# Moving weight splits, a residual and a few row splits to other places in a two-block fp32r kernel's issue order

## The chip, the cores and the metric

One core of a Trainium2 chip runs the whole program. The metric is the device time of one execution in microseconds (us); lower is better. Three runs of the kernel before took 2922.98, 2934.39 and 2939.07 us, so the time before is the median, 2934.39 us.

## What is computed

256 tokens of width 1024 go through two transformer blocks in float32. Block one has, in each of two layers, a SwiGLU feed-forward (`x = x + 0.5 * gate * swiglu(h)`, inner width 2816), a mixer (differential attention, then a gated recurrence) and a second feed-forward. Each normed input is scaled and shifted by columns that come from a conditioning vector:

```python
h = rms_norm(x, norm_g[layer, 0]) * (1.0 + scale[:, :, 0]) + shift[:, :, 0]
x = x + 0.5 * gate[:, :, 0] * swiglu(h, ffn_w_in[layer, 0], ffn_w_down[layer, 0])
```

Block two has a sliding-window attention, an expert layer over 16384 experts (each expert is a row of `u` and a row of `v`), a gated short convolution and a second expert layer. The ten stages are called ffn00, attn1, ffn01, ffn10, hgrn, ffn11, attn2, peer0, conv, peer1.

## The kernel before, in words

**Products.** x lies transposed, features on the partitions, in eight slices `xt[:, k]` of 128 features by 256 tokens. Each weight matrix comes in pieces of 128x1024 elements (512 KB). A piece is loaded by a DMA of SyncE's queue into a `raw` buffer and split into two fp32r halves: `whi`, a copy on ScalarE (ACT), and `wlo = raw - whi` on VectorE (DVE). The input is split in the same way into `xh` and `xl`. A product of one 128x128 block is three matmuls into one PSUM bank: whi by xh, whi by xl, wlo by xh (`mm3`, lines 652 to 657). `features` (898 to 911) multiplies one piece with all eight slices (24 matmuls) and gives one bank; `group` (802 to 812) does that for several pieces at once, slice by slice.

**When a piece is split.** Program order is fixed as the Python runs, and each engine works its instructions off in that order. `take(name, i)` (595 to 606) hands out the next piece. Before, it calls `proc_next` for as long as the pieces split are at most `self.ahead` past the one taken and there is a free pair of buffers. A feed-forward stage has six of those pairs, so with `ahead = 100` the pieces up to number c + 5 are split at the taking of piece c. Pieces are counted from 0 in each stage. `proc_next` (570 to 593) also works off what the plan puts between the pieces: the columns of the conditioning (the `ada_scr` operation on DVE, one per column of 128 values). In ffn00, ffn01 and ffn10 the plan has two of these to three pieces from piece 8 on, in ffn01 and ffn10 in the order 8, ada, 9, ada, 10, 11, ada, 12, ada, 13; ffn11 has none.

**Entering a stage of block one.** `enter` (864 to 884) computes the first six pieces while the norm is still being worked out. Pieces 0 to 3 are multiplied with the unnormed input (258 columns, two of them for the shift); meanwhile the sum of squares, the reciprocal root and its row `rs` are made, and with piece 3 the normed input is written slice by slice over the unnormed one (`norming`, 837 to 862). Pieces 4 and 5 use the normed input. `ahead` takes the four values of `AHEAD` in turn. With `AHEAD[3] = 1` the pieces 0 to 6 are split by the time that `group` has taken 4 and 5. After it `complete` (827 to 835) finishes the four unnormed products (`un`: a multiply and a copy on DVE, an add on ACT).

**The feed-forward.** `ffn` (968 to 1003) then makes the gated products of f = 0, 1, 2 (`glu`: silu on ACT into `sa`, the product `t` on DVE, its split `gh` on ACT and `gl` on DVE), and goes on with pieces 6 and 7 for f = 3 and so on. The banks go round: four for `features`, so piece n may start when the product of piece n - 4 has been read, and pieces 6 to 9 when the `un` of pieces 0 to 3 have been made.

**The residual behind a mixer.** `out_proj` (913 to 949) takes the last two pieces together and ends in `resids` (791 to 800), which for each of eight slices adds to `xt` (DVE), makes the unnormed `xh` (ACT) and `xl` (DVE), squares on ACT and adds the squares on DVE (`ss`). `rstd` (814 to 819) then has four short matmul records sum `ss` over the partitions. At the start of the program `squares_pe` (764 to 773) does it in another way: each squared slice goes to the PE by itself.

**The expert layer.** `peer` multiplies all 128 pieces of `u`, then takes the activations in `slots`, split by `halves` (663) into the eight buffers of `xh` and `xl`, as the input of the 128 pieces of `v`. The first four of these splits (`make(4)`, `make` at 1875) stand behind the last piece of `u`.

Of the kernel before, what the change touches and what calls it, by code (L numbers as in the profile page):

```python
# [19 lines left out]
T = 256  # L20
D = 1024
KD = D // P
# [61 lines left out]
LAST = 2  # L84
PEER_LAST = 3

AHEAD = (2, 3, 3, 1)

STAT = 4

# [248 lines left out]
def moving(pool, n, name):  # L339

    t = pool.tile([P, MOVE + n * T], F32R, name=name)
    return t[:, MOVE:].rearrange("p (a b) -> p a b", b=T)


class Kernel:
# [445 lines left out]
    def resids(self, acc, gate):  # L791

        y = lambda n: acc[n // 2][:, (n % 2) * T:(n % 2 + 1) * T]
        self.add(0, y(0), gate)
        for n in range(KD):
            if n < KD - 1:
                self.add(n + 1, y(n + 1), gate)
            if self.next is not None:
                self.unnormed(n)
                self.squares(n)  # L800

    def group(self, names, cols, role, each=None):

        w = [self.take(*x, n) for n, x in enumerate(names)]
        ps = [self.bank(role) for _ in names]
        for k in range(KD):
            if each is not None:
                each(k)
            for (h, l), p in zip(w, ps):
                self.mm3(p[:, :cols], h[:, k], l[:, k], self.xh[:, k, :cols], self.xl[:, k, :cols],  # L810
                         k == 0, k == KD - 1)
        return ps

    def rstd(self):
# [49 lines left out]
    def enter(self, names, dest):  # L864


        found = []

        def statistics(k):
            if k == STAT:  # L870
                found.append(self.rstd())
            elif k == KD - 1:
                self.rstd_rows(found[0])

        self.ahead = AHEAD[0]
        ps = self.group(names[:2], self.cols, "e", statistics)
        self.ahead = AHEAD[1]
        ps.append(self.features(*names[2], self.cols, "e"))
        self.ahead = AHEAD[2]
        normed = self.norming()  # L880
        ps.append(self.features(*names[3], self.cols, "e", each=normed))
        self.ahead = AHEAD[3]
        two = self.group(names[4:6], T, "n")
        self.ahead = 100
        return [self.complete(p, d) for p, d in zip(ps, dest)] + two
# [82 lines left out]
    def ffn(self, s):  # L968
        nc, wk = self.nc, self.wk
        layer, sub = SUB[s]  # L970
        self.banks(p=range(4), x=range(4, 8), e=range(4), n=[4, 5], ms=[6, 7])
        with self.tc.tile_pool(name=s, bufs=1) as pool:
            gh = moving(pool, KF, "gh")
            gl = moving(pool, KF, "gl")

            def glu(f, pa, pb):
                sa = pool.tile([P, T], F32, name="sa", bufs=2)
                nc.scalar.activation(sa, pa[:, :T], AF.Silu)
                g = wk.tile([P, T], F32, name="t", bufs=3)
                nc.vector.tensor_mul(g, sa, pb[:, :T])  # L980
                self.halves(gh[:, f], gl[:, f], g)

            un = [pool.tile([P, T], F32, name="un", bufs=4) for _ in range(4)]
            first = self.enter([(s + "_in", i) for i in range(6)], un)
            for f in range(3):
                glu(f, first[2 * f], first[2 * f + 1])
            for f in range(3, KF):
                pa = self.features(s + "_in", 2 * f)
                pb = self.features(s + "_in", 2 * f + 1)
                glu(f, pa, pb)  # L990
            nc.scalar.preload_act_table_set(LN_EXP)
            gt = self.gate(layer, sub, 0.5)
            if self.next is not None:
                self.lead(self.next)
            py = {}
            for i, (j, k) in enumerate(DOWN):
                if i % 8 == 0:
                    h, l = self.take(s + "_dn", i // 8)
                if k == 0:
                    py[j] = self.bank("x")  # L1000
                self.mm3(py[j][:, :T], h[:, i % 8], l[:, i % 8], gh[:, k], gl[:, k], k == 0, k == KF - 1)
                if k == KF - 1:
                    self.resid(j, py[j][:, :T], gt)
# [577 lines left out]
    def peer(self, s):  # L1581
# [3 lines left out]
        NJ, WAIT = 128, 1000.0  # L1585
        self.banks(p=range(4), x=range(4, 8), acc=range(4, 8), e=[4, 5, 6] if i == 0 else [1, 2, 3], ms=[7])
        with tc.tile_pool(name=s, bufs=1) as pool, tc.tile_pool(name=s + "g", bufs=2) as self.gp:
# [26 lines left out]
            nh, nl = (moving(spent, KD, n) for n in ("nh", "nl"))  # L1614
# [13 lines left out]
            first = self.group([(s + "_q", hp) for hp in range(3)], T, "e")  # L1628
# [157 lines left out]
            state = dict(j=0, t=0)  # L1786
# [16 lines left out]
            def steps():  # L1803
                yield from choose()
                state["chosen"] = True
                yield from build()
# [4 lines left out]
            def work(us):  # L1811
                credit[0] += us
                while credit[0] > 0.0:
                    c = next(gen, None)
                    if c is None:
                        return
                    if c == WAIT:
                        credit[0] = 0.0
                        return
                    credit[0] -= c  # L1820
# [15 lines left out]
            def slot(j):  # L1836
                j = ORDER[j]
                return slots[:, j] if j < P - N_SHARED else state["shared"][:, j - (P - N_SHARED)]

            def activate(j, ps):  # L1840
                t, x = state["t"], slot(j)
                if t < T:
                    nc.scalar.activation(x[:, t:], ps[:, t:T], AF.Gelu)
                if t:
                    e = wk.tile([P, T], F32, name="t", bufs=3)
                    nc.scalar.activation(e[:, :t], ps[:, :t], AF.Gelu)
                    v.tensor_mul(x[:, :t], x[:, :t], e[:, :t])
                state["j"] = j + 1

            for j in range(NJ):  # L1850
                work(BUDGET)
                while j >= J_FREE and "chosen" not in state:
                    work(1.0)
                if j == N_FREE - 3:
                    self.more = {}
                if j == N_FREE + 1:
                    assert max(max(self.parts[k, True]) for k in ("whi", "wlo")) < self.n_live
                    stack.close()
                    shared = stack.enter_context(tc.tile_pool(name=s + "s", bufs=1))
                    state["shared"] = shared.tile([P, N_SHARED, T], F32, name="shared")  # L1860
                    self.ahead = 100
                if 0 < j < 5:
                    for k in (2 * j - 2, 2 * j - 1):
                        nc.scalar.activation(self.xh[:, k, :T], nh[:, k].bitcast(F32), AF.Copy)
                        v.tensor_copy(self.xl[:, k, :T], nl[:, k].bitcast(F32))
                ps = self.features(s + "_u", j, x=(nh, nl) if j < 5 else None)
                self.after(2, lambda j=j, ps=ps: activate(j, ps))
                self.tick()
            while state["t"] < T:
                work(1.0)  # L1870
                self.tick()
            acc = [self.bank("acc") for _ in range(4)]
            made = [0]

            def make(upto):
                while made[0] < min(upto, NJ):
                    j = made[0]
                    self.halves(self.xh[:, j % 8, :T], self.xl[:, j % 8, :T], slot(j))
                    made[0] += 1

            def part(n, j, w):
                self.mm3(acc[n // 2][:, (n % 2) * T:(n % 2 + 1) * T], w[0][:, n], w[1][:, n],
                         self.xh[:, j % 8, :T], self.xl[:, j % 8, :T], j == 0 and n % 2 == 0, j == NJ - 1, skip=True)

            make(4)
            for j in range(NJ - PEER_LAST):
                self.tick()
                if j == 4:
                    self.drain()
                    nc.scalar.preload_act_table_set(LN_EXP)  # L1890
                if j == NJ // 2:
                    stack.close()
                    parts(PEER_LAST)
                make(j + 4)
                w = self.take(s + "_v", j)
                for n in range(KD):
                    part(n, j, w)
            if self.next is not None:
                self.lead(self.next)
            make(NJ)  # L1900
            w = [self.take(s + "_v", NJ - PEER_LAST + i, i) for i in range(PEER_LAST)]
            for n in range(KD):
# [9 lines left out]
    def build(self):  # L1912
# [5 lines left out]
        self.psum = pool("psum", 1, space=bass.MemoryType.PSUM)  # L1918
        self.banks(x=[4, 5, 6, 3], ms=[7])
        ctx.enter_context(tc.manual_schedule())  # L1920
        self.make_plan()
        self.ada_done = set()

# [35 lines left out]
        s = self.stages[0]  # L1959
# [114 lines left out]
```

## Time and profile before

| | us |
|---|---|
| median of three runs | 2934.39 |
| lowest, highest run | 2922.98, 2939.07 |
| the profiled execution, its own time | 2930.7 |
| its span, first to last instruction | 2928.9 |
| PE busy in the span | 2853.0 (97%) |
| DVE busy | 2177.9 (74%) |
| ACT busy | 1670.7 (57%) |

The profiled execution took 1.8 us more than its span, and 3.7 us less than the median. A matmul's record lasts about 0.28 us, but in a stream they start every 0.11 to 0.12 us, so a busy PE is an upper bound; how far apart they start tells more. In the timelines a row has the start, the duration, the engine, the operation, what is written and read, how many instructions are merged, and in brackets the idle time of the engine before it and what ended it.

### The profile page before, as it was taken

To read this page: it belongs to the slowest core of one execution; us is meant where nothing else is said; L and a number is where in the kernel's file an instruction comes from. 1 tells how busy PE (TensorE), PEld (TensorE's weight loads), DVE (VectorE), ACT (ScalarE), POOL (GpSimd) and SP (SyncE) were. 2 spreads that over 40 slices of the span, in tenths; PEclk is the share of its full clock that TensorE was granted. 3 is DMA by queue.
4 is the path that set the end of the run, shared out by engine and by line. 5 is a ranking of instruction groups with operands and counts; after the bars stand their busy time and mean duration, and the time that the engine had idled before them with its cause. 6 is when DMAs were issued, how large, how long until landed. Compare 5 with 4: busy or idle time off the path is not lost.

```text
span 2928.9 us, 61184 instructions
## 1 busy us (share of the span) xinstructions
PE 2853.0 (97%) x24416; PEld 2806.1 (96%) x24416; DVE 2177.9 (74%) x4491; ACT 1670.7 (57%) x3234; POOL 12.2 (0%) x20
## 2 busy tenths in 40 slices
PE   4999989999999999999999999999999999999999
PEld 4998889999999999799999999999999999999999
DVE  6876778878797655779889755656779889755554
ACT  4455654455465544664688655555464688654543
POOL 0000000000000000000000000000000000000000
PEclk9999999999999999999999999999999999999999
DMA  6984459879643554155544555656445544555654
GB/s 253 341 320 173 152 188 331 278 259 326 231 149 127 188 187 157 54 171 194 184 163 161 173 193 194 216 195 212 163 166 187 188 161 165 173 187 186 207 187 142
DMA packets 158990, 577.17 MB, mean 197 GB/s; under 512 B 17648, under 2 KB 19824, under 8 KB 158320
## 3 DMA queue, kind: packets, MB, share of 16 engines
q1 hardware_dynamic: 156096, 565.25, 56.4%
q0 software_dynamic: 1280, 6.30, 0.6%
q8 instruction: 191, 3.13, 0.4%
q10 hardware_dynamic: 1328, 1.71, 0.2%
q14 instruction: 95, 0.78, 0.1%
HBM read 570.57 MB, written 2.62 MB: 196 GB/s over the span
## 4 chain that ended last, share of the span: by engine, by line
PE 92%; DVE 4%; ACT 2%; issue 1%; DMA 1%; ACTq 0%; DVEq 0%
PE bank L249 92%; DVE wlo L249 1%; DVE xl L249 1%; ACT whi L249 1%; DVE t L249 1%; DMA params<-par 1%; ACT L249 0%; ACT un L249 0%; DVE ada_scr L249 0%; DVE ss L249 0%; DMA raw<-ffn_in 0%; DMA raw<-attn_qk 0%; ACT xh L249 0%; ACT gh L249 0%; ACT pk L249 0%
## 5 line engine op out<-in xcount | busy, mean ns | idle before, releaser
L249 PE MATMUL bank<-xh,whi 128*128 128x256 f32 (+1 forms) x6272 | 1775.9, 283 | 26.1 <-ACT whi L249 17.3
L249 PE MATMUL bank<-xh,wlo 128*128 128x256 f32 (+1 forms) x6272 | 1752.9, 279 | 4.0 <-DVE wlo L249 4.0
L249 PE MATMUL bank<-xl,whi 128*128 128x256 f32 (+1 forms) x6272 | 1755.8, 280 | 0.5
L249 DVE TENSOR_TENSOR wlo<-raw,whi 128x1024 fp32r<-128x1024 f32 x932 | 1134.3, 1224 | 540.5 <-ACT whi L249 532.7
L249 ACT ACTIVATE whi<-raw 128x1024 fp32r<-128x1024 f32 x932 | 973.3, 1057 | 704.0 <-PE bank L249 610.9
L249 PEld LDWEIGHTS bank<-xh,whi 128*128 128x128 f32 x6272 | 1187.9, 189 | 32.3 <-ACT whi L249 18.5
L249 PEld LDWEIGHTS bank<-xl,whi 128*128 128x128 f32 x6272 | 1194.4, 190 | 6.5 <-DVE xl L249 2.1
L249 PEld LDWEIGHTS bank<-xh,wlo 128*128 128x128 f32 x6272 | 1188.0, 189 | 5.4 <-DVE wlo L249 5.4
L249 PE MATMUL bank<-gh,whi 128*128 128x256 f32 x704 | 196.1, 278 | 0.0
L249 PE MATMUL bank<-gl,whi 128*128 128x256 f32 x704 | 196.1, 278 | 0.0
L249 PE MATMUL bank<-gh,wlo 128*128 128x256 f32 x704 | 196.1, 278 | 0.0
L249 DVE SCALAR_TENSOR_TENSOR ada_scr<-raw,cact 128x1024 f32<-128x1024 f32 x144 | 175.5, 1219 | 8.4 <-ACT cact L249 6.2
L249 ACT ACTIVATE ql<-q,gl 128x128 f16<-128x128 f16 x512 | 162.5, 396 | 0.0
L249 ACT ACTIVATE gh<-t 128x256 fp32r<-128x256 f32 x88 | 36.8, 418 | 190.7 <-DVE t L249 190.7
L249 PEld LDWEIGHTS bank<-gh,wlo 128*128 128x128 f32 x704 | 132.9, 189 | 0.0
L249 PEld LDWEIGHTS bank<-gl,whi 128*128 128x128 f32 x704 | 132.9, 189 | 0.0
L249 PEld LDWEIGHTS bank<-gh,whi 128*128 128x128 f32 x704 | 132.2, 188 | 0.0
L249 ACT ACTIVATE slots<-bank 128x256 f32<-128x256 f32 (+38 forms) x296 | 86.8, 296 | 16.7 <-PE bank L249 16.3
L249 PE MATMUL bank<-oh,whi 128*128 128x256 f32 x256 | 73.8, 288 | 0.2 <-ACT hx L249 0.2
L249 PE MATMUL bank<-qh,pm 128*128 128x128 f16 x512 | 73.0, 222 | 0.3
L249 PE MATMUL bank<-ql,pm 128*128 128x128 f16 x512 | 71.5, 219 | 0.1
L249 PE MATMUL bank<-ol,whi 128*128 128x256 f32 x256 | 71.6, 280 | 0.0
(235 smaller groups left out, 2551.4 us busy)
## 6 DMA issues: line engine op xcount, KB each, us to landing
raw<-peer_u SPq DMA_DIRECT2D x256, 512.0 KB, 3.3
raw<-peer_v SPq DMA_DIRECT2D x256, 512.0 KB, 3.4
raw<-ffn_in SPq DMA_DIRECT2D x176, 512.0 KB, 5.1
raw<-ada SPq DMA_DIRECT2D x144, 512.0 KB, 5.3
raw<-ffn_dn SPq DMA_DIRECT2D x88, 512.0 KB, 5.0
raw<-peer_q SPq DMA_DIRECT2D x32, 512.0 KB, 3.3
raw<-conv_in SPq DMA_DIRECT2D x24, 512.0 KB, 4.3
raw<-attn_qk SPq DMA_DIRECT2D x16, 512.0 KB, 4.7
```

The source lines that it names most:

```text
L249: result = real(*args, **kw)
```

## The change

It sets `AHEAD[3]` to 2. It gives the banks of a feed-forward stage in another order. It issues `glu(1)` and `glu(2)` behind the first piece of f = 3 and f = 4. Where a feed-forward follows a mixer, `resids` only adds slice 0 and leaves a function `feed`; `group` calls it in front of each slice of the stage's first two pieces, and the squares go to the PE slice by slice; the row `rs` is then made within piece 2. In the expert layer the first four rows of `v` are split within the last piece of `u`.

```diff
-AHEAD = (2, 3, 3, 1)
+AHEAD = (2, 3, 3, 2)
...
         self.add(0, y(0), gate)
+        if self.next is not None and self.next[0] == "f":
+            def feed(n):
+                if n < KD - 1:
+                    self.add(n + 1, y(n + 1), gate)
+                self.unnormed(n)
+                if n:
+                    self.squares_pe(n - 1)
+
+            self.feed, self.ss = feed, None
+            return
         for n in range(KD):
...
         w = [self.take(*x, n) for n, x in enumerate(names)]
         ps = [self.bank(role) for _ in names]
+        feed, self.feed = self.feed, None
         for k in range(KD):
+            if feed is not None:
+                feed(k)
             if each is not None:
                 each(k)
...
+        if feed is not None:
+            self.squares_pe(KD - 1)
         return ps
...
+        def rows(k):
+            if k == STAT:
+                self.rstd_rows(found[0])
+
         self.ahead = AHEAD[0]
-        ps = self.group(names[:2], self.cols, "e", statistics)
+        ps = self.group(names[:2], self.cols, "e", None if fed else statistics)
+        if fed:
+            found.append(self.rstd())
         self.ahead = AHEAD[1]
-        ps.append(self.features(*names[2], self.cols, "e"))
+        ps.append(self.features(*names[2], self.cols, "e", each=rows if fed else None))
...
-        self.banks(p=range(4), x=range(4, 8), e=range(4), n=[4, 5], ms=[6, 7])
+        self.banks(p=[2, 3, 0, 1], x=range(4, 8), e=[2, 3, 0, 1], n=[5, 7], ms=[4, 6])
...
-            for f in range(3):
-                glu(f, first[2 * f], first[2 * f + 1])
+            glu(0, *first[0:2])
             for f in range(3, KF):
                 pa = self.features(s + "_in", 2 * f)
+                if f < 5:
+                    glu(f - 2, *first[2 * f - 4:2 * f - 2])
                 pb = self.features(s + "_in", 2 * f + 1)
                 glu(f, pa, pb)
...
+            def early(k):
+
+                if state["t"] == T and k < 4:
+                    make(k + 1)
+
...
-                ps = self.features(s + "_u", j, x=(nh, nl) if j < 5 else None)
+                ps = self.features(s + "_u", j, x=(nh, nl) if j < 5 else None, each=early if j == NJ - 1 else None)
```

## Rows read from the trace of the kernel before

**Rows 1.** The page: the chain that ended last, by engine.
```profile
PE 92%; DVE 4%; ACT 2%; issue 1%; DMA 1%; ACTq 0%; DVEq 0%
```

**Rows 2.** The chain in order of time (start, us, what) behind five stage entries.
```profile
72.23 174.30 PE bank L249 x1480
...
423.65 174.88 PE bank L249 x1464
...
619.90 171.68 PE bank L249 x1493
...
806.46 113.92 PE bank L249 x868
...
974.73 186.73 PE bank L249 x1574
```

**Rows 3.** Timeline of PE in ffn10: piece 7 starts, then piece 12.
```profile
618.64 0.38 PE L249 MATMUL bank<-xh,whi 128*128 128x256 f32 x1 [4.06 <-ACT whi L249]
...
634.78 0.28 PE L249 MATMUL bank<-xh,whi 128*128 128x256 f32 x1
```

**Rows 4.** Timeline of ACT in ffn10.
```profile
609.28 0.51 ACT L249 ACTIVATE xh<-t,shift 128x256 fp32r<-128x256 f32 x1 [0.41 <-DVE t L249]
...
617.54 1.99 ACT L249 ACTIVATE whi<-raw 128x1024 fp32r<-128x1024 f32 x2
```

**Rows 5.** Timeline of DVE in ffn10.
```profile
610.29 0.42 DVE L249 TENSOR_TENSOR un<-bank,ss 128x256 f32<-128x256 f32 x1
...
618.62 2.36 DVE L249 TENSOR_TENSOR wlo<-raw,whi 128x1024 fp32r<-128x1024 f32 x2 [0.52 <-ACT whi L249]
620.89 1.22 DVE L249 SCALAR_TENSOR_TENSOR ada_scr<-raw,cact 128x1024 f32<-128x1024 f32 x1
```

**Rows 6.** Timeline of PE: piece 12 starts in ffn00, ffn01, ffn11.
```profile
87.83 0.28 PE L249 MATMUL bank<-xh,whi 128*128 128x256 f32 x1
...
439.75 0.28 PE L249 MATMUL bank<-xh,whi 128*128 128x256 f32 x1
...
990.13 0.28 PE L249 MATMUL bank<-xh,whi 128*128 128x256 f32 x1
```

**Rows 7.** Stretches: us, busy (x count) of PE, PEld, DVE, ACT, POOL; PEclk, DMA, GB/s.
```profile
619.50:622.90 3.40, 3.00 (x14) 3.00 (x15) 3.40 (x5) 2.87 (x4) 0.00 (x0) 0.50 0.51 188
...
807.20:810.60 3.40, 3.40 (x18) 3.40 (x18) 1.80 (x3) 2.95 (x5) 0.00 (x0) 0.50 0.85 275
```

**Rows 8.** Timelines between hgrn and ffn11: DVE, ACT, SP, PE.
```profile
939.74 0.87 DVE L249 SCALAR_TENSOR_TENSOR xt<-bank,gate,xt 128x256 f32<-128x256 f32 x2
...
957.03 0.87 DVE L249 SCALAR_TENSOR_TENSOR t<-xt,gain,ss 128x256 f32<-128x256 f32 x2
...
948.05 1.99 ACT L249 ACTIVATE whi<-raw 128x1024 fp32r<-128x1024 f32 x2
...
950.22 0.20 ACT L249 ACTIVATE rsq<-rsq 128x2 f32<-128x2 f32 x1
...
939.85 0.33 SPq L249 DMA_DIRECT2D raw<-ffn_in  x1
...
948.81 0.61 PE L249 MATMUL bank<-ones_d,ss 128*128 128x1 f32 x4 [3.12 <-DVE ss L249]
949.28 0.36 PE L249 MATMUL bank<-xh,whi 128*128 128x258 f32 x1
```

**Rows 9.** DMA issues from 933 to 946 us: KB each, median us to landing.
```profile
raw<-ffn_in SPq DMA_DIRECT2D x8, 512.0 KB, 4.1
```

**Rows 10.** Timeline of PE in hgrn (piece 7) and attn1 (piece 8).
```profile
805.20 0.39 PE L249 MATMUL bank<-xh,whi 128*128 128x256 f32 x1 [0.91 <-ACT whi L249]
...
273.21 0.58 PE L249 MATMUL bank<-xh,whi 128*128 128x256 f32 x1 [4.89 <-ACT hx L249]
```

**Rows 11.** Timeline of PE where peer0 goes from u to v.
```profile
1685.75 0.28 PE L249 MATMUL bank<-xh,whi 128*128 128x256 f32 x1
1686.16 0.38 PE L249 MATMUL bank<-xl,whi 128*128 128x256 f32 x1
```

More of the change, by code (lines that the diff above doesn't have):

```diff
@@ L864, in enter @@
     def enter(self, names, dest):
+        fed = self.feed is not None
         found = []
@@ L1848, in activate, with make @@
                 state["j"] = j + 1
+            made = [0]
+            def make(upto):
+                while made[0] < min(upto, NJ):
+                    j = made[0]
+                    self.halves(self.xh[:, j % 8, :T], self.xl[:, j % 8, :T], slot(j))
+                    made[0] += 1
+            def early(k):
+                if state["t"] == T and k < 4:
+                    make(k + 1)
             for j in range(NJ):
@@ L1872, in peer @@
             acc = [self.bank("acc") for _ in range(4)]
[L1873 to L1879, printed above, removed]
             def part(n, j, w):
@@ L1920, in build @@
         ctx.enter_context(tc.manual_schedule())
+        self.feed = None
         self.make_plan()
```

## The prediction, made before the change was run

> **What bounds the kernel now.** I began with the page's chain of waits, the work that ended last followed back: 92% of it is PE [rows 1]. In order of time it falls into long unbroken runs of matmuls: 1493 of them follow 619.90 in 171.68 us [rows 2], one each 0.115 us, so a piece of 24 takes about 2.75 us wherever PE is fed. What is to be won lies at the stage entries where a run breaks, and there I read the timelines engine by engine. In ffn10 piece 7 starts after an idle 4.06 us, released by its `whi` [rows 3], because ACT reaches that copy only at 617.54, behind the gated products, though the last normed slice was done at 609.79 [rows 4]; its `wlo` starts at 618.62 and ends about 1.2 us later [rows 5]. Behind the wait comes a second loss: for 3.4 us the granted clock is 0.50, which is 1.2 GHz, half of the upper level [rows 7]. Only 14 to 18 matmuls start there instead of some 29, about 1.7 us. Such an entry stands in ffn00, ffn01, ffn10 and ffn11, a smaller one (0.91 us, then 0.50 as well) in hgrn [rows 7, 10]. At the mixer's end PE waits 3.12 us for the last sum `ss` [rows 8].
>
> The sum below is on the profiled execution, 2930.7 us, 1.8 us over its span and 3.7 us under the median of the runs, 2934.39. I add the change to the median.
>
> **Part 1, piece 7 split early, products spread (four feed-forward entries).** I walk the two queues in ffn10. `whi` of piece 7 goes to 609.7-610.7 and `wlo` to 610.8-612.0. The first `un`, at 610.29 before [rows 5], thus moves by some 1.7 us, to 612.0, and piece 6, which needs its bank, waits under 1 us. Only `glu(0)` is left in front of piece 8: its `wlo` starts near 617.8 where before it was the second of the pair from 618.62, at 619.8 [rows 5], so the 4.06 us become about 0.9 at piece 8. So far this looks like nearly all won. But work is only moved on DVE, and DVE has six operations in its queue next: `wlo` of 8, a column of conditioning, 9, a column, 10, 11, each some 1.14 us apart (1.22 us long, overlapping) [rows 5]. The product `t` of `glu(1)`, which the change puts behind the first piece of f = 3, stands behind all six: 617.8 + 6.8 = 624.6. On ACT its `gh` waits for that `t`, and behind `gh` in ACT's order stand `whi` of 12 (1.0 us, half of [rows 4]) and the silu of f = 3, which frees the bank that piece 10 needs: 626.8. Piece 10 then waits about 2.5 us, and after two pieces more PE waits again, some 1.6 us, for the silu of f = 4. By this walk piece 12 starts at 633.95, against 634.78 before [rows 3]: a gain of 0.8 us only. DVE's backlog is late next, in place of ACT's `whi`.
>
> In the other entries I measure from the chain's break to piece 12: in ffn10 after the change 633.95 - 619.90 = 14.05 us. The two stages with the same two columns to three pieces get the same: ffn01 423.65 + 14.05 = 437.70 against 439.75, a gain of 2.05; ffn00 72.23 + 14.05 = 86.28 against 87.83, a gain of 1.55 [rows 2, 6]. ffn11 has no columns, so four of 1.22 us leave DVE's queue before piece 12 and the walk has it at 985.1 against 990.13 [rows 6]: 5.0. Together **-9.4 us**. The bounds: 0, if DVE's queue is longer than I count, and four times the stall and its slow clock, 4 x (4.06 + 1.7) = -23, if it never bites. I take the walk because each of its operations has a row.
>
> The new order of the banks costs nothing that I can find, as long as piece 6 follows the `un` of the bank it gets; the wait of under 1 us above is that.
>
> **Part 2, the residual in the first products (ffn01, ffn11).** Before, `resids` came whole, then the splits of pieces 2 and 3 (`whi` from 948.05) [rows 8]. Now `take` runs inside `group` right behind `add` of slice 0 and in front of all the rest. In ffn11 the raw of piece 3 was issued only at 939.85 and lands about 3.3 to 4.1 us later (the window's median is 4.1) [rows 8, 9], so `whi` runs 943.2-944.2, `wlo` to 945.4, and the second `add`, which stood at 940.2, waits behind it on DVE; on ACT `xh` of slice 0 waits behind `whi`. The first `xl` is ready at 946.3. From there the group is PE's own: 48 matmuls of 0.12 us and eight groups of sums, each of four short records. One such group took 0.47 us (948.81 to 949.28) [rows 8]. 48 x 0.12 + 8 x 0.47 = 9.6 us, ends 955.9. Behind it comes the root on ACT and DVE (before, 1.1 us from the sums' end at 949.28 to 950.42) [rows 8], the `whi` and two `wlo` of the next pieces (1.0 + 2.36 [rows 4, 5]) and then the first normed `t`: 960.3 against 957.03 before [rows 8], **+3.3**. The one wait of 3.12 us is gone, but another of about 3.7 us stands ahead of the group. After a wait of that size the clock fell to 0.50 elsewhere [rows 7], and here the slower stretch then lies under the longer group: +1.5 us. In sum +4.8 in each of the two stages, **+9.6**. ffn01 takes the same for lack of a nearer row; there only piece 3 is to be split. Bounds in each: -0.8 (below) and +5.6, with a landing of 4.1 instead of 3.3.
>
> The short records could be cheaper or dearer. The trace says 0.118 us each, as much as a matmul with 256 columns, and the sum uses that. The Trainium skill (TensorE: Matmul & The Clock Gate, Back-to-back issue gap) gives a moving side of 1 to 64 columns a floor of about 25 ns; by that a group would be an estimated 0.1 us and the two stages 5.9 us shorter.
>
> **Part 3, hgrn.** Piece 7 is split early there too, and no long DVE queue of conditioning lies behind it: 0.91 us of wait and 1.7 of slow clock go [rows 7, 10]: **-2.6** (bounds 0 and -2.6). **attn1**: PE waits 4.89 us for `hx` ahead of piece 8 [rows 10]; the extra early `wlo` (1.2 us) pushes it somewhat, bounds 0 and +1.2, I take a third, **+0.4**. attn2, conv and the query products keep their waits. **Part 4, v's first rows:** from u to v PE steps 0.41 us where it is usually 0.11 [rows 11]. Made within the last piece of u, ready on time, that is 0.3 to 0.4 in each expert layer: **-0.8** (bounds 0, -0.8).
>
> **Sum:** -9.4 + 9.6 - 2.6 + 0.4 - 0.8 = **-2.8 us**. So 2927.9 on the profiled scale, **2931.6** as a median. My own range for this case, by the bounds, is about 2919 to 2942. A measurement of this kernel can tell about 0.5% from no change, 14.7 us: faster is under 2919.7, slower over 2949.1.
>
> **Rivals.**
> (a) DVE's backlog does not bite, and the splits land ahead of the second `add`: all four stalls vanish with their slow clock, -23.2; hgrn -2.6, v -0.8; in each fed stage the 3.12 us wait and its 1.5 us go and 3.8 us of sums come, -0.8, two times -1.6. Sum -28.2, 2906.2. For: DVE is 74% busy overall. Against: six operations in a row at that place [rows 5]. Chance 0.15.
> (b) Only the residual goes well (raw of piece 3 already there): -9.4 - 1.6 - 2.6 + 0.4 - 0.8 = -14.0, 2920.4. For: the transfer may be issued earlier when buffers come free earlier. Chance 0.12.
> (c) Only the entries go well: -23.2 + 9.6 - 2.6 + 0.4 - 0.8 = -16.6, 2917.8. Chance 0.09.
> (d) Slower. In the fed stages the wait ahead of the group brings the clock down and PE, fed slice by slice, does not get it back through the two first pieces and piece 2. At 0.50 a matmul takes about 0.21 us (3.0 us busy for 14) [rows 7] instead of 0.12: 72 x 0.09 + 3.8 for the sums at half speed = 10.3, two times 20.6; 3.0 of it were in the forecast: -2.8 + 20.6 - 3.0 = +14.8, 2949.2. It decides if 0.50 lasts more than 10 us behind a wait. Against: the stretches that I see last 3.4. Chance 0.06.
> (e) A record with one moving column costs PE almost nothing, since it waits only for its issue: the 2 x 8 groups of 0.47 us [rows 8] drop out, 7.5 at most: -2.8 - 7.5 = -10.3, 2924.1. The row speaks against it. The Trainium skill's floor, named above, is this mechanism; the same page's section LDWEIGHTS (loading the stationary operand), where the price goes by the 128 columns loaded, an estimated 107 ns by its formula, agrees with the 118 ns of the row instead. Chance 0.03.
> That leaves 0.50 for the forecast and 0.05 for what I don't see.
>
> **Numbers.** Faster: (a) 0.15, half of (b) and (c), each near the bound, 0.11, and 0.04 of the rest: 0.30. Slower: half of (d) and some of the unseen, 0.05. Same 0.65. The range from 2906 to 2944 holds the forecast, (b), (c), (e) and half of (a).
>
> **What would show it.** Right: no wait on `whi` at piece 7; instead PE idle ahead of piece 10, released by ACT's silu, behind a `gh` that waits for a `t` of DVE. `wlo` of piece 3 between the first two `add`s of ffn11, and a first `xl` near 946. First normed `t` some 3 us later behind the chain's start, 32 short records in it. hgrn without a 0.50 stretch at its entry. Wrong: piece 12 in ffn10 more than 3 us earlier against the last normed slice; short records that start less than 0.05 us apart; the group starting within 1 us of the mixer's last matmul; a clock of 0.50 for longer than 4 us.

## The result and the profile after the change

The changed kernel took 2948.36 us (median of 20 runs, 2936.32 to 2962.48), the kernel before 2923.73 us (20 runs, 2905.24 to 2941.16). The ratio is **1.0082, with a 95% interval of 1.0059 to 1.0105**: 24 us slower. 2931.6 us had been forecast, 2.8 us less than the median of before that was known then. The profiled execution took 2955.93 us, its span is 2954.2 us, 25.3 us over the span of before.

The page of the changed kernel answers to [rows 1]:

```profile
span 2954.2 us, 61280 instructions
...
PE 92%; DVE 3%; ACT 3%; issue 1%; DMA 1%; ACTq 0%; DVEq 0%
```

The chain is as before, 92% PE. So the 25 us are mostly time in which PE works, not time in which it waits, and one has to ask how fast it works. I took PE's starts at the borders of the stages from both timelines and set the difference beside the forecast's terms:

| stretch | forecast, us | difference of the two profiles, us |
|---|---|---|
| ffn00 | -1.55 | -1.74 |
| attn1 | +0.4 | +0.26 |
| ffn01, from the mixer's end to piece 4 | +4.8 | +11.06 |
| ffn01, piece 4 to piece 12 | -2.05 | -2.63 |
| ffn01, the rest | 0 | -5.75 |
| ffn10 | -0.8 | -0.87 |
| hgrn | -2.6 | -1.43 |
| ffn11, from the mixer's end to piece 4 | +4.8 | +11.80 |
| ffn11, piece 4 to piece 12 | -5.0 | -5.05 |
| ffn11, the rest | 0 | +0.11 |
| attn2 | 0 | +6.06 |
| peer0 and peer1 | -0.8 | +13.74 and -0.3 |

Three sorts of rows stand out. The entries came as worked out. The two fed groups cost more than twice the forecast. And there are stretches that the forecast had at nothing or nearly so (the rest of ffn01, attn2, peer0), with both signs, where the same instructions ran at another pace.

**The fed groups.** PE's timeline at the entry of ffn11 after the change, which answers to the PE lines of [rows 8]:

```profile
941.42 0.28 PE L249 MATMUL bank<-oh,wlo 128*128 128x256 f32 x1
944.24 0.39 PE L249 MATMUL bank<-xh,whi 128*128 128x258 f32 x1 [2.54 <-ACT xh L249]
946.08 0.58 PE L249 MATMUL bank<-xl,whi 128*128 128x258 f32 x1 [1.45 <-DVE xl L249]
946.46 0.42 PE L249 MATMUL bank<-xh,wlo 128*128 128x258 f32 x1
946.67 0.42 PE L249 MATMUL bank<-xh,whi 128*128 128x258 f32 x1
...
947.32 0.85 PE L249 MATMUL bank<-ones_d,sq 128*128 128x1 f32 x4
948.02 0.56 PE L249 MATMUL bank<-xh,whi 128*128 128x258 f32 x1
...
963.05 0.56 PE L249 MATMUL bank<-xh,whi 128*128 128x258 f32 x1
```

DVE's timeline there:

```profile
942.87 2.36 DVE L249 TENSOR_TENSOR wlo<-raw,whi 128x1024 fp32r<-128x1024 f32 x2 [4.08 <-ACT whi L249]
945.15 0.48 DVE L249 SCALAR_TENSOR_TENSOR xt<-bank,gate,xt 128x256 f32<-128x256 f32 x1
945.55 0.48 DVE L249 SCALAR_TENSOR_TENSOR xl<-xt,gain,xh 128x256 fp32r<-128x256 f32 x1
```

The start is as forecast: the two splits stand on DVE ahead of the second `add`, and the first `xl` is ready at 946.0 (946.3 had been worked out). From there no wait is left on PE. But matmuls start every 0.215 us and a group of four short records (the sum of one slice's squares, one moving column each) takes 0.71 us. The stretches of the changed kernel show the clock there (us; busy time and count of PE, PEld, DVE, ACT, POOL; granted clock; DMA share, GB/s):

```profile
395.00:413.00 18.00, 18.00 (x86) 18.00 (x85) 5.29 (x14) 6.58 (x16) 0.00 (x0) 0.50 0.28 112
946.00:966.00 20.00, 19.92 (x93) 19.93 (x94) 7.28 (x19) 8.20 (x19) 0.00 (x0) 0.50 0.32 129
628.30:631.60 3.30, 3.30 (x18) 3.30 (x17) 2.82 (x4) 1.63 (x3) 0.00 (x0) 0.50 1.02 406
1219.00:1242.50 23.50, 22.92 (x88) 14.94 (x89) 13.08 (x59) 9.90 (x38) 0.00 (x0) 0.50 0.00 1
```

In the fed group of ffn11 (second row) PE is busy for 19.92 of 20 us and still has a granted clock of 0.50, 1.2 GHz. It comes back to 2.4 GHz at 966.16, 3.1 us behind the last short record. The first row is the fed group of ffn01, the third is the entry of ffn10 (below). The last is attn2 (0.50 there from 1218.75 to 1242.64, before from 1213.39 to 1223.63), which the change doesn't touch.

**The entries.** PE and ACT in ffn10 after the change, against [rows 3, 4]. PE:

```profile
620.24 0.39 PE L249 MATMUL bank<-xh,wlo 128*128 128x256 f32 x1 [0.58 <-DVE wlo L249]
...
627.94 0.38 PE L249 MATMUL bank<-xh,whi 128*128 128x256 f32 x1 [2.19 <-ACT sa L249]
```

ACT:

```profile
621.68 0.40 ACT L249 ACTIVATE sa<-un 128x256 f32<-128x256 f32 x1
626.25 0.42 ACT L249 ACTIVATE gh<-t 128x256 fp32r<-128x256 f32 x1 [4.18 <-DVE t L249]
626.58 1.04 ACT L249 ACTIVATE whi<-raw 128x1024 fp32r<-128x1024 f32 x1
627.52 0.36 ACT L249 ACTIVATE sa<-bank 128x256 f32<-128x256 f32 x1
```

This is the walk of part 1: no wait at piece 7 any more, but piece 10 waits for the silu, which stands behind a `gh` that waits 4.18 us for a `t` in DVE's queue. It waits 2.19 us where about 2.5 had been worked out. The second wait of the walk, 1.6 us ahead of piece 12, is not in this trace: behind piece 10's wait the clock is at 0.50 for 3.4 us (the row 628.30:631.60 above), and the slower matmuls fill the time until the silu of f = 4 has freed the bank. Experiment 7 below has the same entry with the clock at 1.00; there PE waits 2.01 and then 1.35 us for the silu, and from piece 4 to piece 12 it takes 28.95 us against 29.05 here.

**peer0.** Two stretches of the products with v, one of the kernel before and one of the changed kernel:

```profile
1800.00:1830.00 30.00, 30.00 (x267) 30.00 (x267) 17.24 (x24) 15.04 (x22) 0.00 (x0) 1.00 0.60 193
```

```profile
1800.00:1830.00 30.00, 30.00 (x257) 30.00 (x256) 16.78 (x22) 14.51 (x22) 0.00 (x0) 1.00 0.56 193
```

Same instructions, PE always busy, clock 1.00 in both, and 267 records against 257. The spacing, the time from one start to the next, is 113.3 ns on average in the one and 117.8 ns in the other, through some 3170 matmuls without a break: about 14 us. The switch stands at the step from u to v, which answers to [rows 11]:

```profile
1697.57 0.28 PE L249 MATMUL bank<-xh,whi 128*128 128x256 f32 x1
1697.68 0.35 PE L249 MATMUL bank<-xl,whi 128*128 128x256 f32 x1
1697.87 0.28 PE L249 MATMUL bank<-xh,wlo 128*128 128x256 f32 x1
```

PE still waits a little, for `xl`: a step of 0.19 us in place of 0.41. Ahead of it the spacing is 113.3, behind it 117.8. In ffn01 (-5.75) it is the other way round: 117.8 in the kernel before, 113.3 in the changed one.

### The profile page after: what moved, and what is told of

The parts are those of the page before. It is cut to its first block, busy times and chain, and to the rows that moved or that the text cites. A ratio compares the mean times of both kernels' runs of the same rounds, so it can differ in the third digit from the quotient of the medians.

```text
span 2954.2 us, 61280 instructions
## 1 busy us (share of the span) xinstructions
PE 2885.3 (98%) x24472; PEld 2833.3 (96%) x24472; DVE 2173.7 (74%) x4477; ACT 1665.9 (56%) x3234; POOL 12.2 (0%) x20
## 4 chain that ended last, share of the span: by engine, by line
PE 92%; DVE 3%; ACT 3%; issue 1%; DMA 1%; ACTq 0%; DVEq 0%
PE bank L249 92%; ACT whi L249 1%; DVE wlo L249 1%; DVE t L249 1%; DMA params<-par 1%; DVE ada_scr L249 1%; DVE xl L249 0%; ACT L249 0%; ACT un L249 0%; ACT xh L249 0%; ACT hx L249 0%; DMA raw<-attn_qk 0%; ACT pk L249 0%; ACT sa L249 0%; ACT hsq L249 0%
## 5 line engine op out<-in xcount | busy, mean ns | idle before, releaser
L249 PE MATMUL bank<-xh,whi 128*128 128x256 f32 (+1 forms) x6272 | 1784.6, 285 | 24.7 <-ACT xh L249 7.3
L249 ACT ACTIVATE slots<-bank 128x256 f32<-128x256 f32 (+38 forms) x296 | 86.4, 294 | 16.8 <-PE bank L249 16.7
L249 PE MATMUL bank<-oh,wlo 128*128 128x256 f32 x256 | 72.3, 282 | 0.0
```

Source lines behind the costliest of these rows:

```text
L249: result = real(*args, **kw)
```

## The experiments

The theories at this point: (T1) the fed groups lose their time to the low clock, and it takes two things, a wait that brings the clock down and the short records that keep it there; (T2) the length or place of the hold between u and v (a step longer than the usual spacing) decides at which spacing v runs; (T3) the rest of the 25 us, attn2 and the feed-forward streams, is drawn anew, that is, differs between executions of one program. Rivals: the feeding itself is slow; all of it is drawn; the hold matters for nothing but its own length. Each kernel ran 12 times (11 in experiment 6, six in 8 and 10). The kernel before ran beside them, and each ratio is to those runs, with its 95% interval in brackets. Experiments 1 to 4 ran on one chip, 5 to 8 on a second, 9 and 10 on a third. The quoted text in each was written before the run.

**1. Without the fed residual.**

```diff
-        if self.next is not None and self.next[0] == "f":
+        if self.next is not None and self.next[0] == "-":
             def feed(n):
```

> The changed kernel with the residual made whole again in front of the first products (part 2 undone), the rest of the change kept. Theory: in the changed kernel PE ran at a granted clock of 0.50 for 20.5 us in each of the two fed groups, and from the mixer's end to the sixth piece these cost 11.1 and 11.8 us more than before. Without them the time falls by about 20 us against the changed kernel, to some 4 us either side of the kernel before (the entries gain 10 us in the profiles, rates of the long streams permitting). Rival: most of the 25 us lie in the spacing of the long matmul streams (113.3 or 117.8 ns at full clock), drawn anew in every kernel; then it stays 10 us or more above before.

Measured: 2925.62 us, ratio 1.0021 (0.9998 to 1.0044). Against the changed kernel's 1.0082 that is 18 us, known to some 10 us by the two intervals. From the mixer's end to piece 4 it took 19.3 us in ffn01 and 18.6 in ffn11, against 27.8 and 29.3. The fed groups are the larger part, though the kernel is not yet below before. In ffn01 19.3 us is more than the 16.7 in the profile of before, for the same residual: here the clock is at 0.50 for 6.8 us from within the wait for `ss` on. The profiles of experiments 5, 6 and 9, which have that residual too, show 19.0 to 19.8 us and the same 6.8 us at 0.50. So the one profile of before was a lucky execution there, and some 2 to 3 of ffn01's +11.06 us come from that.

**2. v's first rows behind u again.**

```diff
-..., each=early if j == NJ - 1 else None)
+...)
```

> The changed kernel with the first four rows of v split behind the last piece of u again (part 4 undone). Theory: the step from u to v is 0.41 us again instead of 0.19 to 0.30, and that is all: 0.4 us in two layers, within 2 us of the changed kernel. Rival: the length of this hold decides at which of the two spacings the 3200 matmuls of v then run; at 113.3 instead of 117.8 ns a layer is 14 us shorter, so the time falls by 14 (one layer) or up to 28 us (both), and the profile shows the spacing of v at 113.3 in at least one layer.

Measured: 2937.08 us, ratio 1.0050 (1.0029 to 1.0071), some 9 us under the changed kernel, which the two intervals only just tell from nothing. The step is 0.41 us again and peer0's v runs at 113.3 ns; peer1's stays at 117.8. My theory here (within 2 us) was the wrong one; the rival, with 14 us for one layer, came nearer.

**3. Squares summed on DVE, one sum behind the group.**

```diff
                 if n:
-                    self.squares_pe(n - 1)
+                    self.squares(n - 1)
...
-            self.feed, self.ss = feed, None
+            self.feed = feed
...
         if feed is not None:
-            self.squares_pe(KD - 1)
+            self.squares(KD - 1)
```

> The changed kernel, residual still made slice by slice in the first products, but the squares are summed on DVE as before and go to PE once behind the group; the 32 short records in the group are gone. Theory: the short records between the slices keep PE at 1.2 GHz once a wait has brought it there; without them the 0.50 stretch lasts no more than 3.4 to 7 us, the group takes about 8 us from its first xl instead of 17, and the time falls by 2 x 9 = 18 us. Rival: it is the wait at the start and the feeding by ACT and DVE that keep the clock down; the stretch lasts as long (over 15 us) and the time falls only by the records' own 2 x 5.7 us or less.

Measured: 2931.61 us, ratio 1.0019 (0.9993 to 1.0046), 18 us under the changed kernel. Its stretches at the entry of ffn11:

```profile
934.50:941.30 6.80, 5.39 (x25) 5.19 (x25) 6.80 (x18) 4.68 (x12) 0.00 (x0) 0.50 0.99 398
941.40:944.50 3.10, 3.10 (x29) 3.10 (x27) 2.22 (x6) 1.20 (x4) 0.00 (x0) 1.00 0.37 151
```

The wait in front is the same (2.54 and 1.41 us), the clock falls as well, but without the records it is back at 1.00 after 6.8 us, not 20.5. To piece 4 it takes 18.5 and 19.4 us, 9 to 10 less than in the changed kernel.

**4. The splits of pieces 2 and 3 behind the feeding of slices 2 and 4.**

```diff
+        feed, self.feed = self.feed, None
+        if feed is not None:
+            self.ahead = 0
         w = [self.take(*x, n) for n, x in enumerate(names)]
...
-        feed, self.feed = self.feed, None
+        c0 = self.n_take
...
                 feed(k)
+                if k in (2, 4):
+                    while self.n_w <= c0 + (k == 4) and self.room() and self.proc_next():
+                        pass
```

> The changed kernel with the splits of pieces 2 and 3 taken out from in front of the residual: they are issued behind the feeding of slices 2 and 4. The 32 short records stay. Theory: the wait of 2.5 plus 1.4 us in front of the group falls under 1.5 us, and whether the clock then stays at 2.4 GHz tells if the wait or the records matter: with no fall the group takes 48 x 0.12 + 8 x 0.47 = 9.6 us and the time drops by 2 x 10 = 20 us. Rival: the records bring the clock down by themselves; the 0.50 stretch is there without a long wait and the time drops by the 2 to 3 us of shorter wait in each stage, 5 us.

Measured: 2929.97 us, ratio 1.0016 (0.9990 to 1.0043), 19 us under the changed kernel. PE in ffn11:

```profile
931.08 0.28 PE L249 MATMUL bank<-oh,wlo 128*128 128x256 f32 x1
931.20 0.28 PE L249 MATMUL bank<-xh,whi 128*128 128x258 f32 x1
...
931.92 0.50 PE L249 MATMUL bank<-ones_d,sq 128*128 128x1 f32 x4
932.29 0.36 PE L249 MATMUL bank<-xh,whi 128*128 128x258 f32 x1
```

Its stretch from the mixer's end to piece 4:

```profile
931.10:947.80 16.70, 16.19 (x136) 15.81 (x134) 11.49 (x22) 10.82 (x21) 0.00 (x0) 1.00 0.73 259
```

No wait, all 32 records, and the clock stays at 1.00. So neither the wait alone (experiment 3) nor the records alone (experiment 4) hold the clock down for longer than 6.8 us; together they do. Four records take 0.37 us here. To piece 4 it takes 15.8 and 16.7 us, under the 16.7 and 17.5 in the profile of before: fed in this order the residual is worth about 1 us a stage against that profile, and 3 to 4 us in ffn01 against the 19.0 to 19.8 of the other four.

After these four, T1 held, but entries that gain 10 us in the profiles should have put kernels 1, 3 and 4 below before. All three have v's rows early. The next four take the parts alone or leave that one out.

**5. The entries alone** (residual and v as before; the two edits of experiments 1 and 2 together).

```diff
-        if self.next is not None and self.next[0] == "f":
+        if self.next is not None and self.next[0] == "-":
...
-..., each=early if j == NJ - 1 else None)
+...)
```

> Parts 1 and 3 alone: AHEAD, the order of the banks and the spread products; residual and v as before. Theory: the entries gain what the profiles show (ffn00 1.7, ffn01 2.6, ffn10 0.9, ffn11 5.0, hgrn 1.4 us) and nothing is lost, so the time is about 10 us below the kernel before (ratio near 0.9965), and about 10 below the kernel without the fed residual that still had v's rows early (1.0021). Rival: the entries' gain is eaten elsewhere and the ratio is 1.000 to 1.002, like that kernel's.

Measured: 2906.53 us beside 2913.11 of before, ratio 0.9973 (0.9955 to 0.9990): faster by 8 us.

**6. v's rows early, alone on the kernel before.**

```diff
...
-                ps = self.features(s + "_u", j, x=(nh, nl) if j < 5 else None)
+                ps = self.features(s + "_u", j, x=(nh, nl) if j < 5 else None, each=early if j == NJ - 1 else None)
```

> Part 4 alone on the kernel before: v's first four rows split within the last piece of u. Theory (the shorter step from u to v lets the stream of peer0 settle at 117.8 ns more often): ratio 1.002 to 1.005, 6 to 14 us slower, and the profile shows peer0's v at 117.8. Rival (the step matters for nothing but its own length): 0.5 us faster, ratio within 0.002 of 1.

Measured: 2932.04 us, ratio 1.0049 (1.0023 to 1.0075): 14 us slower, by an edit that shortens a wait. The profile did not show v at 117.8: the profiled execution, 2909.49 us, is one of the three quick ones among eleven (2909.20, 2909.49, 2915.07), and has 113.3 in both layers. The other eight lie from 2924 to 2938; of the 28 runs of before beside them four do. So the slow spacing in these eight is inferred from the times and from the profiles of other kernels, not seen here.

**7. Experiment 4 with v's rows behind u** (its diff and this one).

```diff
-..., each=early if j == NJ - 1 else None)
+...)
```

> The changed kernel with the splits of pieces 2 and 3 behind the feeding of slices 2 and 4, and v's rows behind u as before. Theory: with the slow clock and the early rows both gone the entries' 10 us and 1 to 2 us of the fed residual are left: 10 to 12 us below the kernel before, ratio 0.996. Rival: 1.0016 as with the early rows.

Measured: 2902.64 us, ratio 0.9964 (0.9941 to 0.9986), as the theory had it, and 15 us under experiment 4 by the ratios.

**8. The same, and the columns of conditioning from piece 13 on.**

```diff
-ADA_RATE = {"ffn00": 0.67, "attn1": 0.5, "ffn01": 0.67, "ffn10": 0.67, ...
+ADA_RATE = {"ffn00": 0.78, "attn1": 0.5, "ffn01": 0.78, "ffn10": 0.78, ...
...
-            if count[s] > 8:
+            if count[s] > (13 if s[0] == "f" else 8):
```

> As the one before, and the columns of conditioning in the feed-forward stages begin at piece 13 instead of 8, a little denser (0.78 to a piece instead of 0.67). Theory (DVE's columns between pieces 8 and 12 are what is late next in ffn00, ffn01 and ffn10): the wait ahead of piece 10 (2.4 us) and the slow clock behind it go in these three, the stretch from the fifth piece to piece 12 falls from 28.5 to 29 us to the 25.0 us that ffn11 has without columns, in sum 10 us more: ratio 0.993. Rival: DVE is late later instead (denser columns) or the columns pile up ahead of a stage that needs them, and nothing is won against the kernel with the columns from piece 8.

Measured: 2887.11 us, ratio 0.9916 (0.9889 to 0.9942). From piece 4 to piece 12 it took 24.7, 25.9 and 25.6 us in ffn00, ffn01 and ffn10, against 27.0, 29.2 and 29.0 in the kernel of experiment 7; ffn11, without columns, stays at 25.8. The wait ahead of piece 10 (2.0 to 2.2 us in experiment 7) is gone in all three. That shows DVE's columns to be what was late next. The three make 8.9 us. By the ratios it is 14 us, and the profiles differ in more, which I had not foreseen: attn1 fell from 151.1 to 142.8 us, its wait for `hx` from 4.88 to 2.06 us and its time at 0.50 from 17.1 to 3.4 us; and the rest of ffn01 ran at 113.3 ns instead of 117.8 (5.7 us). How much of this the edit does and how much is drawn, one profile can't tell.

**9. The kernel before, with buffers of its own for the first row of v, split ahead of the last piece of u.**

```diff
+            def row(j):
+                if j == 0:
+                    vh, vl = state["rows"]
+                    return vh[:, j], vl[:, j]
+                return self.xh[:, j % 8, :T], self.xl[:, j % 8, :T]
...
             for j in range(NJ):
+                if j == NJ - 1 and state["t"] == T:
+                    make(1)
```

> The kernel before, with buffers of its own for the first row of v, which is split ahead of the last piece of u; rows 1 to 3 stay behind u. PE then needs no hold at all between u and v. Theory (a hold in the stream draws the spacing anew, an unbroken stream keeps what it has; u's last pieces run at 113.3 ns): no step over 0.13 us between u and v, v at 113.3 in both layers, 0.8 us off for the two holds and no runs in a cluster 14 or 28 us up: ratio 0.995 to 0.9995, and a narrower spread than that of the kernel with the early rows (2909 to 2938). Rival (splitting early brings the slower spacing, whatever the hold, by its work on ACT and DVE beside the last piece): v at 117.8 in peer0 and a ratio near 1.005, as with the early rows.

Measured: 2910.78 us, ratio 0.9983 (0.9964 to 1.0003), runs from 2904 to 2920. PE at the step from u to v, and a stretch of v:

```profile
1681.57 0.28 PE L249 MATMUL bank<-xh,wlo 128*128 128x256 f32 x1
1681.68 0.28 PE L249 MATMUL bank<-vh,whi 128*128 128x256 f32 x1
1681.79 0.28 PE L249 MATMUL bank<-vl,whi 128*128 128x256 f32 x1
```

```profile
1800.00:1830.00 30.00, 30.00 (x267) 30.00 (x266) 17.24 (x23) 15.12 (x23) 0.00 (x0) 1.00 0.59 197
```

No hold at all, the 113.3 ns of u go on through v in both layers, and the slower cluster of experiment 6 is gone, though a row is still split early. That speaks for the hold and against the splitting's own work, but it doesn't show it: one row is split here and four there, the chip is another, and experiments 5, 7 and 8 kept 113.3 in both layers behind the hold of 0.41 us. The time is that of before.

**10. Experiments 8 and 9 together** (both diffs).

> The fastest so far (fed residual with late splits, columns from piece 13, v's rows behind u) and the first row of v in buffers of its own. Theory: as above, 0.8 us and no draw at the step from u to v: ratio 0.988 to 0.9915. Rival: the slower spacing comes and the ratio is 0.996 or more.

Measured: 2881.86 us beside 2912.08, ratio **0.9885 (0.9858 to 0.9911)**: 30 us under the kernel before. Both layers run at 113.3, as in experiments 5 to 9.

The parts add up as far as that was tried: entries 0.9973 (experiment 5) and early rows 1.0049 (experiment 6) give -0.0027 + 0.0049 = +0.0022, and the kernel with both (experiment 1) measured 1.0021. The fed residual has no run of its own; what it adds is the changed kernel over that one, 1.0082 / 1.0021 = 1.0061.

## Why the prediction was wrong

**Parts 1 and 3 were right in their mechanism.** The entries' terms were -9.4 for the feed-forwards, -2.6 for hgrn and +0.4 for attn1, -11.6 in sum. The profiles show -10.3, -1.4 and +0.3, and experiment 5, which has them alone, measured 8 us, with the interval from 3 to 13. The stall moved to piece 10, behind DVE's queue, and experiment 8 confirmed the cause. That the sum came within 1 us in the profiles is helped by luck: the feed-forwards gave 0.9 us more than their term and hgrn 1.2 less.

**Part 2 had the right start and the wrong clock.** This is the step that failed first. The wait of about 3.7 us was foreseen (4.0 measured in ffn11, 2.7 in ffn01), and that the clock would fall behind it. The sentence "the slower stretch then lies under the longer group: +1.5 us" put its length at the 3.4 us of [rows 7], where a plain stream of matmuls of 256 columns followed the wait. Here eight groups of short records stood in the stream, and 0.50 lasted 20.5 us: from the first `xl` to piece 2 the group took 17.0 us, not the 9.6 plus 1.5 of the sum. In the profiles the term is +11.1 and +11.8 instead of +4.8 each; as a whole, by the ratios, 18 us instead of 9.6. It is rival (d), which had a chance of 0.06. Its 2949.2 us lies near the measured median by luck: it was added to a median of before that was 11 us too high, and it had nothing for v's rows. Its "against" was that the slow stretches that I see last 3.4 us. That was misread. Two of the four entries in the trace of before, ffn00 and ffn01, have 0.50 for 6.8 us, and attn1, at the very wait of 4.89 us that the prediction cites [rows 10], has it for 13.65 us, with short records (two moving columns) between the matmuls:

```profile
70.00:76.80 6.80, 5.37 (x23) 5.08 (x24) 6.28 (x8) 5.92 (x7) 0.00 (x0) 0.50 0.48 131
...
421.50:428.30 6.80, 5.45 (x23) 5.15 (x24) 6.28 (x9) 5.96 (x7) 0.00 (x0) 0.50 0.55 157
```

```profile
271.30:285.00 13.70, 11.79 (x55) 11.79 (x56) 5.83 (x15) 7.16 (x17) 0.00 (x0) 0.50 0.66 242
```

```profile
275.72 1.71 PE L249 MATMUL bank<-halves_w,hsq 128*128 128x2 f32 x8
277.29 0.56 PE L249 MATMUL bank<-xh,whi 128*128 128x256 f32 x1
```

So a wait with short records behind it, and more than 10 us at 0.50, could be read before the change was run. attn2, where small matmuls ran at 0.50 for 10 us, is another.

The price of the records themselves was not the trouble. A group takes 0.37 us at the upper clock (experiment 4) where I used 0.47, that is 0.092 us a record. The row that I used had run at the end of a wait. Rival (e), by which a record costs almost nothing, is out. The 25 ns that the Trainium skill gives (TensorE: Matmul & The Clock Gate, Back-to-back issue gap) are, as that section says, for an isolated matmul without the load of its weights, and are not met here. The 92 ns are nearer to the estimated 107 ns that the Trainium skill's formula for loading 128 columns gives (TensorE: Matmul & The Clock Gate, LDWEIGHTS (loading the stationary operand)).

**Part 4 had the wrong sign.** It was priced as a wait alone, -0.8 us with bounds 0 and -0.8. The upper bound was wrong, because the stream behind the wait was taken to be the same with and without it. In the trace of before both spacings can be seen, 113.3 in peer0's v and 117.8 in peer1's, behind the same hold of 0.41 us. I had reckoned with one pace, 0.115 us on average. It is two levels, and a layer of v is worth 14 us between them. Alone the part measured +14 us (experiment 6); taken out of three other kernels it gave back 9 (experiment 2), 14 (experiment 1 against 5) and 15 us (4 against 7). That the spacing of v is how it costs this is likely but not shown in every kernel. Where peer0's v ran at 113.3 in spite of the early rows, the profiled execution was a quick one: 15 us under its kernel's median in experiment 3, 23 in 6. Where it ran at 117.8 (experiments 1 and 4) it was within 4 us of the median.

**The range** ended at 2944 and the median was 2948.36. The bounds of the terms add up to -28 and +12.4 us, that is 2906 to 2947, not to the 2919 to 2942 that the prediction calls its own range; even they leave the result out. The forecast had been added to 2934.39, a median of three runs; over 20 runs the kernel before stands at 2923.73. On that scale the forecast of -2.8 is 27 us off: 8 from the fed groups, 15 from v's rows, 4 from the entries, each known to 5 to 10 us.

What stays open: how a hold settles the spacing. With v's rows early, peer0's v ran at 117.8 in the profiles of the changed kernel and of experiments 1 and 4, and at 113.3 in those of 3 and 6, behind the same step of 0.19 us. With the hold of 0.41 it ran at 113.3 in all five profiles, and peer1's v still had 117.8 in the profile of before and in that of experiment 2. So the hold does not fix the spacing; the runs fit that it changes how often each comes. One rival is not settled, the chip: peer1's v ran at 117.8 in all four profiles of experiments 1 to 4 and at 113.3 in all six of 5 to 10, behind holds of 0.41, of 0.19 and of none alike, and of the runs of before beside them 15 of 35 took 2924 us or more on the first chip, 4 of 28 and 2 of 17 on the others. What part 4 cost in experiment 6 is not touched by that, since before ran beside it on the same chip. attn2's +6.06 is no part of the change: 0.50 lasts 24 us there in experiment 9 too, which has neither fed residual nor new entries, and 10 us in experiment 10, which has both.

## What to carry to other kernels

When PE is the bound, a wait's price is not only its length: ask at which clock and which spacing the stream runs behind it, and look for both levels in the trace before an edit is costed at a few tenths of a us. In this kernel it was wrong to put short matmuls into a stream that starts behind a wait: see to the wait first (here by issuing two weight splits later), or keep the short ones out until the clock is back. A stall that is removed on one engine is only gone if the next queue has room; moving DVE's side work out of that place was worth about as much as the move itself (8.9 us in the profiles, where the entries had made 10.3). And one profile of a kernel is one draw: clock and spacing in the same stretch differed between executions by several us here, so take a stretch's time from more than one.

## What the runs showed of the hardware that I had not expected

A PE that is busy for 19.92 of 20 us can stay at a granted clock of 0.50. Here a wait came first (4.0 us in ffn11, 2.7 in ffn01) and groups of four short records (one moving column) stood between the matmuls, in both fed groups for 20.5 us. Without the wait the same records left the clock at 1.00 (experiment 4); with the wait and without the records it was back after 6.8 us (experiment 3).

At a granted clock of 1.00 one and the same stream of matmuls has two steady spacings, 113.3 and 117.8 ns. It keeps one for 360 us without a break and changes at a step as small as 0.07 us over the usual. With no step at all (experiments 9 and 10) it kept 113.3 in all four layers seen, but so it did in all eight of experiments 5 to 8, behind steps of 0.19 and 0.41 us. What chooses the level is open.
